# Weight tiles that are a matmul's stationary operand begin 64 bytes further into their buffers

## The chip, the cores and the metric

The kernel runs on one core of a Trainium2 chip. The metric is the device time of one execution in microseconds (us), the median over the runs.

## What is computed

Two transformer blocks over 256 tokens of width 2048, in float32. The first has a stick-breaking attention branch and a latent attention branch with gates, then a feed-forward layer; the second has an attention layer and a retention layer. Nearly all work is multiplying 256 tokens by weight matrices, one after the other:

```python
proj = rms_norm(h, norm_pre_mix) @ w_in                      # 2048 x 8512
q = rms_norm(q_lat, q_norm) @ w_uq;  kv = rms_norm(kv_lat, kv_norm) @ w_ukv
mixed = (g_sb * (sb @ w_o_sb) + g_mla * (mla @ w_o_mla)) @ w_out
gu = rms_norm(h, norm_pre_ffn) @ w_gate_up;  h = h + rms_norm((silu(g) * up) @ w_down)
proj = h @ attn_w_in;  x = layer_norm(ALPHA * x + (o * silu(g)) @ attn_w_out)
proj = x @ ret_w_in;   x = layer_norm(ALPHA * x + (o * silu(g)) @ ret_w_out)
```

## The kernel before

Each weight matrix is read once, in units of 2 x 128 rows by up to 512 columns (512 KB). `run` streams the units: `load` has SyncE (its queue is SPq in the rows) issue the transfer into one of 5 `raw` buffers, up to four units ahead; `split`, three units ahead of use, has ScalarE round the unit to float32r (`whi`) and VectorE compute the rest (`wlo`); four buffers each. Activations are split likewise: `u0` and `u1` (both "u" in rows), `osb`, `omh`/`oml`, `lath`/`latl`, `mh`/`ml`, `oh`/`ol`, `roh`/`rol`. Every product is three float32r matmuls, high by high, high by low and low by high (`mm3`), so TensorE has three matmuls for each pair of 128 x 128 blocks, each behind a load of its own stationary block.

There are two ways to multiply. In `gemm_t` the weights are stationary (128 columns of `whi` or `wlo` are loaded) and 256 columns of activations move through the array; the output is transposed. A full unit is 24 matmuls of 256 columns. In `gemm_n` the activations are stationary and 512 columns of weights move; a unit is 12 matmuls of 512 columns. In rows, the name behind the arrow's first place is the moving operand: `g<-u,whi` is `gemm_t`, `g<-whi,u` is `gemm_n`. `gemm_t` makes the q, k and latent projections of `w_in`, both gates, `w_uq`, `w_o_sb`, `w_o_mla`, the gates of the second attention layer and q and k of retention; `ukv_units` uses each weight tile both ways. The rest, above all the feed-forward layer, is `gemm_n`.

The order of instructions on each engine is the order in which the code issues them; `bg_add` tasks (attention heads, norms) are put between units by `bg_step`.

All large tiles begin at a multiple of 256 bytes in their partition. The `whi` buffers stand at bytes 39,424, 43,520, 47,616 and 51,712, `wlo` from 55,808, `u0` at 72,192, `u1` at 88,576, all of them multiples of 512. `omh`, `oml`, `lath` and `latl` (148,224, 156,416, 191,232 and 201,472) lie 256 bytes off one. The slices that a matmul reads are 512 bytes (stationary), 1,024 or 2,048 bytes (moving) long, and begin at multiples of 256 bytes, too, on both sides.

Two temporaries matter. `diag` makes a diagonal from a vector, for the three row norms of the first block (keys x, q and kv); it has two buffers of 1,024 bytes. `sq0` holds sums of squares at the start, in the place tagged `acc`.

Of the kernel before, what the change touches and what calls it, by code (L numbers as in the profile page):

```python
# [10 lines left out]
F32 = mybir.dt.float32  # L11
F32R = mybir.dt.float32r
# [5 lines left out]
P = 128  # L18
S = 256
# [40 lines left out]
def tile_two_blocks(ctx: ExitStack, tc: tile.TileContext, a, out):  # L60
    nc = tc.nc
# [3 lines left out]
    wp = ctx.enter_context(tc.tile_pool(name="wp", bufs=1))  # L65
    mp = ctx.enter_context(tc.tile_pool(name="main", bufs=1))
# [14 lines left out]
    def gbank():  # L81
        return psg.tile([P, 512], F32, tag="g", name="g")
# [4 lines left out]
    def split2(t, n=2):  # L87
        return t.rearrange("p (a b) -> p a b", a=n)

    def f32(t):  # L90
        return t.bitcast(F32)


    def mm3(o, l, r, start, stop):

        mm(o, l[0], r[0], start, False)
        mm(o, l[0], r[1], False, False)
        mm(o, l[1], r[0], False, stop)

    def mm(o, l, r, start, stop):  # L100
        pe.matmul(out=o, lhsT=l, rhs=r, start=start, stop=stop, skip_group_check=True)  # L101

    def copy(o, i, **k):
        act.activation(out=o, in_=i, func=AF.Copy, **k)  # L104
# [10 lines left out]
    def sub(o, x, y, eng=None):  # L115
        tt(o, x, y, ALU.subtract, eng)
# [26 lines left out]
    class Task:  # L143
        def __init__(self, group, stages, gap, after, at):
            self.group, self.stages, self.gap, self.after, self.at = group, deque(stages), gap, after, at
# [25 lines left out]
    def bg_step():  # L171
        clock[0] += 1
        for _ in range(rate[0]):
            bg_fill()
            t = next((t for t in active if t.at <= clock[0] and not pending(t.after)), None)
            if t is None:
                return
            bg_run(t)
# [34 lines left out]
    units = []  # L213

    class Unit:
        __slots__ = ("srcs", "nk", "nc", "use", "after")

        def __init__(self, srcs, nk, ncol, use, after=False):
            self.srcs, self.nk, self.nc, self.use, self.after = srcs, nk, ncol, use, after

    RAW, SPL, AHEAD = 5, 4, 3
    before_load, before_split = {}, {}
    stream, on_pool = {}, set()

# [5 lines left out]
    def run():  # L230
        raws, parts = {}, {}

        def load(i):
            if i >= len(units):
                return
            before_load.pop(i, lambda: None)()
            u = units[i]
            if u.srcs is None:
                return
            t = wp.tile([P, 2, 512], F32, tag="raw", name="raw", bufs=RAW)  # L240
            for k0, k1, c0, c1, src in u.srcs:
                nc.sync.dma_start(out=t[:, k0:k1, c0:c1], in_=src)
            raws[i] = t

        def split(i):
            if i >= len(units):
                return
            before_split.pop(i, lambda: None)()
            u = units[i]
            if u.srcs is None or i not in raws:  # L250
                return
            t = raws.pop(i)[:, 0:u.nk, 0:u.nc]
            hi = wp.tile([P, 2, 512], F32R, tag="whi", name="whi", bufs=SPL)
            lo = wp.tile([P, 2, 512], F32R, tag="wlo", name="wlo", bufs=SPL)
            copy(hi[:, 0:u.nk, 0:u.nc], t)
            sub(lo[:, 0:u.nk, 0:u.nc], t, f32(hi[:, 0:u.nk, 0:u.nc]), pool if i in on_pool else dve)
            parts[i] = (hi, lo)

        stream["split"] = split
        for i in range(RAW - 1):  # L260
            load(i)
        for i in range(AHEAD):
            split(i)
        for i, u in enumerate(units):
            stream["at"] = i
            if u.srcs is None:
                u.use(None, None)
            load(i + RAW - 1)
            if u.srcs is not None and drip:
                for f in drip.popleft():  # L270
                    f()
            if not u.after:
                split(i + AHEAD)
            if u.srcs is not None:
                u.use(*parts.pop(i))
                if u.after:
                    split(i + AHEAD)
                elif turns and u.use.__name__ != "held":
                    turn_next()
                bg_step()  # L280

    def wsrc(w, k0, nk, c0, ncol):
        return w[k0 * P:(k0 + nk) * P, c0:c0 + ncol].rearrange("(k p) c -> p k c", p=P)

    def gemm_t(w, koff, kblocks, c0, ncol, rhs, evac, srcs=None, blocks=None, before_last=None, lead=None):

        blocks = blocks or [(i * P, min(P, ncol - i * P)) for i in range((ncol + P - 1) // P)]
        st = {}  # L290

        def use_at(k0, nk):
            def use(hi, lo):
                if k0 == 0:
                    st["ps"] = [gbank() for _ in range((len(blocks) + 1) // 2)]
                if k0 + nk == kblocks and before_last:
                    before_last()
                def out_w(b, k):
                    off, m = blocks[b]
                    return (split2(st["ps"][b // 2])[0:m, b % 2, :],  # L300
                            hi[:, k - k0, off:off + m], lo[:, k - k0, off:off + m])

                if k0 == 0 and lead == "w":
                    for x in range(2):
                        for k in range(k0, k0 + nk):
                            for b in range(len(blocks)):
                                o, wh, wl = out_w(b, k)
                                if x:
                                    mm(o, wl, rhs(k)[0], False, False)
                                else:  # L310
                                    mm(o, wh, rhs(k)[0], k == 0 and b % 2 == 0, False)
                                    mm(o, wh, rhs(k)[1], False, False)
                elif lead == "x" and k0 < 4:
                    for k in range(k0, k0 + nk):
                        xh, xl = rhs(k)
                        for b in range(len(blocks)):
                            o, wh, wl = out_w(b, k)
                            mm(o, wh, xh, k == 0 and b % 2 == 0, False)
                            mm(o, wl, xh, False, False)
                        for b in range(len(blocks)):  # L320
                            o, wh, wl = out_w(b, k)
                            mm(o, wh, xl, False, False)
                else:
                    for b in range(len(blocks)):
                        for k in range(k0, k0 + nk):
                            o, wh, wl = out_w(b, k)
                            mm3(o, (wh, wl), rhs(k), k == 0 and b % 2 == 0, k == kblocks - 1)
                if k0 + nk == kblocks:
                    evac(st.pop("ps"))
            return use  # L330

        for k0 in range(0, kblocks, 2):
            nk = min(2, kblocks - k0)
            s = srcs(k0, nk) if srcs else [(0, nk, 0, ncol, wsrc(w, koff + k0, nk, c0, ncol))]
            units.append(Unit(s, nk, ncol, use_at(k0, nk)))

    def gemm_n(w, kblocks, c0, ncol, lhs, evac, koff=0, first=None, last=None):

# [157 lines left out]
    def turn_next():  # L496
        if turns:
            turns.popleft()()
# [17 lines left out]
    def small(name, w=2, bufs=2):  # L516
        return mp.tile([P, w], F32, tag="sm_" + name, name=name, bufs=bufs)

    def diag(r, f):
        dg = mp.tile([P, 2, P], F32, tag="diag", name="diag", bufs=2)  # L520
        stt(dg, ident[:, None, :].to_broadcast([P, 2, P]), f, r[:, :, None].to_broadcast([P, 2, P]),
            ALU.mult, ALU.mult)
        return dg.rearrange("p a b -> p (a b)")
# [10 lines left out]
    def rms_bg(key, get_ps, n, dst):  # L534

        st = {}

        def row():
            v, t = small("v"), small("t")
            st["r"] = small("r", bufs=6)  # L540
            ts(v, get_ps()[:, 0:2], 1.0 / n, ALU.mult, NORM_EPS, ALU.add)
            rsqrt_bg(st["r"], v, t)

        def wide():
            st["d"] = diag(st["r"], 1.0)

        def use():
            o = bbank()
            spread(o, 0, st["d"])
            dst(key, st["r"], o[:, 0:S])  # L550
        return [row, nop, wide, use]
# [20 lines left out]
    p1 = open_phase("p1")  # L572
# [5 lines left out]
    ifr = p1.tile([64, 64], F32, tag="ifr", name="ifr")[:, 0:2]  # L578
    nc.scalar.dma_start(out=cv, in_=a["cv"])
    pool.memset(f32(wz), 0.0)  # L580
    sq0 = p1.tile([P, 2, S], F32, tag="acc", name="sq0")

    copy(small("root"), f32(wz)[:, 0:2])
    warm(22)
# [348 lines left out]
    def ukv_units(p):  # L933
        st = {}
        w = a["w_ukv"]
# [27 lines left out]
                        bg_add("mla%d" % p, mla_head(d, 2 * p + h, h), delay=2)  # L963
            return use
        for k0 in (0, 2):
            units.append(Unit([(0, 2, 0, 512, wsrc(w, k0, 2, p * 512, 512))], 2, 512, use_at(k0)))

    def mla_head(d, head, h):
        st = {}
# [778 lines left out]
```

## Time and profile before

| | |
|---|---|
| median of 3 runs | 2601.6 us (2601.45 to 2601.84) |
| profiled execution, its own time | 2597.73 us |
| its span, first to last instruction | 2595.7 us |
| mean granted clock of TensorE | 0.991 |
| TensorE busy | 2519.6 us (97%) |
| VectorE, ScalarE, GpSimd busy | 1510.1, 1206.2, 232.1 us |
| read from HBM | 458.92 MB, 178 GB/s over the span |

The busy time of TensorE is that of overlapping records: a matmul's record is longer than the distance to the next one's start. How long a matmul keeps the engine is read from the starts.

### The profile page before, as it was taken

To read this page: it belongs to the slowest core of one execution; us is meant where nothing else is said; L and a number is where in the kernel's file an instruction comes from. 1 tells how busy PE (TensorE), PEld (TensorE's weight loads), DVE (VectorE), ACT (ScalarE), POOL (GpSimd) and SP (SyncE) were. 2 spreads that over 40 slices of the span, in tenths; PEclk is the share of its full clock that TensorE was granted. 3 is DMA by queue.
4 is the path that set the end of the run, shared out by engine and by line. 5 is a ranking of instruction groups with operands and counts; after the bars stand their busy time and mean duration, and the time that the engine had idled before them with its cause. 6 is when DMAs were issued, how large, how long until landed. Compare 5 with 4: busy or idle time off the path is not lost.

```text
span 2595.7 us, 36165 instructions
## 1 busy us (share of the span) xinstructions
PE 2519.6 (97%) x14362; PEld 2212.6 (85%) x14362; DVE 1510.1 (58%) x1782; ACT 1206.2 (46%) x1496; POOL 232.1 (9%) x346
## 2 busy tenths in 40 slices
PE   8999999999999999999999899998999999999997
PEld 8999999997778888888888788987889898898785
DVE  7756656556655454445455766766565656565445
ACT  4565554444454444444444445554444444454333
POOL 3012000002000000000000211211110010102000
PEclk9999999999999999999999999999999999999998
DMA  7655555755466666666656454564656556555763
GB/s 228 176 157 157 164 163 174 232 169 180 143 203 187 194 187 193 191 192 193 188 188 194 144 170 146 158 197 156 199 158 184 173 168 185 180 179 156 257 193 115
DMA packets 248889, 465.48 MB, mean 179 GB/s; under 512 B 21328, under 2 KB 31888, under 8 KB 247696
## 3 DMA queue, kind: packets, MB, share of 16 engines
q1 hardware_dynamic: 245312, 448.32, 56.9%
q0 software_dynamic: 2688, 13.63, 1.4%
q8 instruction: 112, 1.84, 0.3%
q10 hardware_dynamic: 720, 1.22, 0.1%
q14 instruction: 57, 0.47, 0.1%
HBM read 458.92 MB, written 4.19 MB: 178 GB/s over the span
## 4 chain that ended last, share of the span: by engine, by line
PE 63%; DVE 3%; POOL 2%; ACT 2%; issue 1%; DMA 1%; POOLq 0%; ACTq 0%; DVEq 0%
PE g L101 60%; PE b L101 2%; DMA raw<-in_ret_w_out_dram 1%; POOL qkraw L107 1%; ACT whi L104 1%; DVE wlo L107 1%; POOL t L107 0%; ACT pp L1357 0%; PE b L1217 0%; POOL z L107 0%; DVE nm L1354 0%; PE b L448 0%; POOL t L417 0%; DVE qkraw L107 0%; PE b L1607 0%
## 5 line engine op out<-in xcount | busy, mean ns | idle before, releaser
L107 DVE TENSOR_TENSOR wlo<-raw,whi 128x1024 fp32r<-128x1024 f32 (+2 forms) x849 | 1053.0, 1250 | 822.8 <-ACT whi L104 817.8
L104 ACT ACTIVATE whi<-raw 128x1024 fp32r<-128x1024 f32 (+2 forms) x852 | 886.9, 1051 | 900.3 <-PE g L101 842.2
L101 PE MATMUL g<-whi,u 128*128 128x512 f32 x3200 | 1009.2, 393 | 0.1
L101 PEld LDWEIGHTS g<-whi,u 128*128 128x128 f32 x3200 | 605.4, 189 | 126.3 <-ACT whi L104 0.6
L101 PE MATMUL g<-wlo,u 128*128 128x512 f32 x1600 | 628.9, 393 | 11.4 <-DVE wlo L107 11.4
L101 PE MATMUL g<-u,whi 128*128 128x256 f32 x3424 | 622.1, 284 | 1.2 <-ACT whi L104 1.2
L101 PEld LDWEIGHTS g<-u,whi 128*128 128x128 f32 x3424 | 532.3, 191 | 2.0 <-ACT whi L104 1.4
L101 PE MATMUL g<-u,wlo 128*128 128x256 f32 x1712 | 483.6, 283 | 8.0 <-DVE wlo L107 8.0
L101 PEld LDWEIGHTS g<-wlo,u 128*128 128x128 f32 x1600 | 303.4, 190 | 76.3 <-DVE wlo L107 15.5
L101 PEld LDWEIGHTS g<-u,wlo 128*128 128x128 f32 x1712 | 326.8, 191 | 9.0 <-DVE wlo L107 9.0
L101 PE MATMUL g<-whi,mh 128*128 128x512 f32 x352 | 137.4, 390 | 0.0
L101 PE MATMUL g<-wlo,mh 128*128 128x512 f32 x352 | 137.0, 389 | 0.0
L101 PE MATMUL g<-whi,ml 128*128 128x512 f32 x352 | 136.0, 389 | 0.0
L101 PE MATMUL g<-wlo,roh 128*128 128x512 f32 x256 | 100.0, 390 | 1.8 <-DVE wlo L107 1.8
L101 PE MATMUL g<-whi,roh 128*128 128x512 f32 x256 | 99.9, 390 | 1.7 <-ACT whi L104 1.7
L101 PE MATMUL g<-whi,rol 128*128 128x512 f32 x256 | 98.7, 389 | 0.0
L107 POOL TENSOR_TENSOR t<-r 128x2 f32<-128x2 f32 (+1 forms) x51 | 21.9, 429 | 654.0 <-DVE r L122 651.3
L101 PEld LDWEIGHTS g<-whi,mh 128*128 128x128 f32 x352 | 66.1, 188 | 13.7
L101 PEld LDWEIGHTS g<-whi,ml 128*128 128x128 f32 x352 | 66.1, 188 | 13.7
L101 PEld LDWEIGHTS g<-wlo,mh 128*128 128x128 f32 x352 | 66.1, 188 | 13.6
L107 POOL TENSOR_TENSOR dacc<-dacc,post_ffn 128x512 f32<-128x512 f32 x6 | 7.6, 1290 | 659.5 <-ACT sqd L438 659.5
L101 PEld LDWEIGHTS g<-wlo,roh 128*128 128x128 f32 x256 | 48.0, 188 | 12.8 <-DVE wlo L107 2.8
(314 smaller groups left out, 2234.5 us busy)
## 6 DMA issues: line engine op xcount, KB each, us to landing
raw<-in_ret_w_in_dram SPq DMA_DIRECT2D x192, 512.0 KB, 4.2
raw<-in_w_gate_up_dram SPq DMA_DIRECT2D x176, 512.0 KB, 3.7
raw<-in_w_in_dram SPq DMA_DIRECT2D x128, 512.0 KB, 4.3
raw<-in_w_down_dram SPq DMA_DIRECT2D x88, 512.0 KB, 4.5
raw<-in_attn_w_in_dram SPq DMA_DIRECT2D x80, 512.0 KB, 3.6
raw<-in_ret_w_out_dram SPq DMA_DIRECT2D x64, 512.0 KB, 4.7
raw<-in_w_out_dram SPq DMA_DIRECT2D x32, 512.0 KB, 4.5
raw<-in_attn_w_out_dram SPq DMA_DIRECT2D x32, 512.0 KB, 4.7
```

The lines of the kernel that those rows point to most:

```text
L101: pe.matmul(out=o, lhsT=l, rhs=r, start=start, stop=stop, skip_group_check=True)
L104: act.activation(out=o, in_=i, func=AF.Copy, **k)
L107: (eng or dve).tensor_tensor(out=o, in0=x, in1=y, op=op)
```

## The change

A weight unit of `gemm_t` or `ukv_units` is split into its `whi` and `wlo` buffers 16 floats, that is 64 bytes, behind the buffer's start. Units of `gemm_n` stay at the start. Each of the eight buffers grows from 4,096 to 4,352 bytes, so that each still begins at a multiple of 256; the 2,048 bytes come from the two `diag` buffers, which now lie in the places of `gate` (key kv) and `sqt` (keys x and q). `sq0` moves into the place of `gate` as well. `u0` and `u1` begin 2,048 bytes later, and all other large tiles stay at multiples of 256. On every engine the same instructions stand in the same order as before; one VectorE multiplication (the first that writes a `gate` tile) waits for one earlier VectorE instruction more.

```diff
     class Unit:
-        __slots__ = ("srcs", "nk", "nc", "use", "after")
+        __slots__ = ("srcs", "nk", "nc", "use", "after", "shift")
...
+    STAT = 16
...
             t = raws.pop(i)[:, 0:u.nk, 0:u.nc]
-            hi = wp.tile([P, 2, 512], F32R, tag="whi", name="whi", bufs=SPL)
-            lo = wp.tile([P, 2, 512], F32R, tag="wlo", name="wlo", bufs=SPL)
+            hi, lo = (wp.tile([P, 1088], F32R, tag=n, name=n, bufs=SPL)[:, u.shift:u.shift + 1024].rearrange(
+                "p (k c) -> p k c", k=2) for n in ("whi", "wlo"))
             copy(hi[:, 0:u.nk, 0:u.nc], t)
...
-            units.append(Unit(s, nk, ncol, use_at(k0, nk)))
+            units.append(Unit(s, nk, ncol, use_at(k0, nk), shift=STAT))
...
-    def diag(r, f):
-        dg = mp.tile([P, 2, P], F32, tag="diag", name="diag", bufs=2)
+    def diag(r, f, tag):
+        dg = p1.tile([P, 2, P], F32, tag=tag, name="diag")
...
-            st["d"] = diag(st["r"], 1.0)
+            st["d"] = diag(st["r"], 1.0, "gate" if key == "kv" else "sqt")
...
-    sq0 = p1.tile([P, 2, S], F32, tag="acc", name="sq0")
+    sq0 = p1.tile([P, 2, S], F32, tag="gate", name="sq0")
...
-            units.append(Unit([(0, 2, 0, 512, wsrc(w, k0, 2, p * 512, 512))], 2, 512, use_at(k0)))
+            units.append(Unit([(0, 2, 0, 512, wsrc(w, k0, 2, p * 512, 512))], 2, 512, use_at(k0), shift=STAT))
```

## Rows read from the trace of the kernel before

**Rows 1.** The page: busy us, share of the span and instructions of each engine.

```profile
PE 2519.6 (97%) x14362; PEld 2212.6 (85%) x14362; DVE 1510.1 (58%) x1782; ACT 1206.2 (46%) x1496; POOL 232.1 (9%) x346
```

**Rows 2.** The chain that ended last: shares of the span by engine.

```profile
PE 63%; DVE 3%; POOL 2%; ACT 2%; issue 1%; DMA 1%; POOLq 0%; ACTq 0%; DVEq 0%
```

**Rows 3.** Groups by form, TensorE: out<-moving,stationary, stationary size, moving size, count | busy us, mean ns.

```profile
L101 PE MATMUL g<-whi,u 128*128 128x512 f32 x3200 | 1009.2, 393 | 0.1
L101 PE MATMUL g<-u,whi 128*128 128x256 f32 x3392 | 616.9, 284 | 1.2 <-ACT whi L104 1.2
L101 PE MATMUL g<-u,wlo 128*128 128x256 f32 x1696 | 479.1, 283 | 8.0 <-DVE wlo L107 8.0
...
L101 PE MATMUL g<-lath,whi 128*128 128x256 f32 x104 | 29.6, 285 | 0.0
...
L101 PE MATMUL g<-u,whi 128*64 128x256 f32 x32 | 5.9, 277 | 0.0
```

**Rows 4.** Timeline, TensorE in a `gemm_t` stretch: start us, us, operation, count.

```profile
517.17 0.28 PE L101 MATMUL g<-omh,wlo 128*128 128x256 f32 x1
517.29 0.40 PE L101 MATMUL g<-u,whi 128*128 128x256 f32 x2
...
518.37 0.40 PE L101 MATMUL g<-u,whi 128*128 128x256 f32 x2
```

**Rows 5.** Timeline, TensorE in a `gemm_n` stretch.

```profile
899.87 0.62 PE L101 MATMUL g<-whi,u 128*128 128x512 f32 x2
...
901.23 0.62 PE L101 MATMUL g<-whi,u 128*128 128x512 f32 x2
```

**Rows 6.** Five stretches: busy us (count) by engine, granted clock, DMA share, GB/s.

```profile
core 0: us, PE busy (x) PEld busy (x) DVE busy (x) ACT busy (x) POOL busy (x), PEclk, DMA share, GB/s
8.00:63.00 55.00, 47.04 (x383) 45.98 (x382) 42.79 (x43) 24.42 (x32) 23.71 (x26) 1.00 0.73 229
517.40:540.20 22.80, 22.80 (x192) 22.80 (x191) 12.11 (x13) 8.44 (x8) 0.00 (x0) 1.00 0.63 187
1844.00:1889.60 45.60, 45.60 (x382) 45.60 (x381) 25.48 (x26) 21.68 (x25) 0.00 (x0) 1.00 0.67 202
980.00:1090.00 110.00, 110.00 (x487) 91.06 (x487) 49.79 (x41) 45.75 (x47) 0.00 (x0) 1.00 0.62 195
688.50:691.50 3.00, 3.00 (x9) 2.35 (x8) 3.00 (x4) 1.99 (x3) 1.88 (x1) 0.50 0.00 0
```

**Rows 7.** Timeline, TensorE in the stretch at half clock.

```profile
688.43 0.63 PE L101 MATMUL g<-wlo,u 128*128 128x512 f32 x1
...
691.42 1.18 PE L101 MATMUL g<-whi,u 128*128 128x512 f32 x4
```

**Rows 8.** Timeline, TensorE where 64 stationary columns are loaded.

```profile
218.45 0.40 PE L101 MATMUL g<-u,whi 128*64 128x256 f32 x2
...
218.80 0.39 PE L101 MATMUL g<-u,whi 128*64 128x256 f32 x2
...
219.14 0.40 PE L101 MATMUL g<-u,whi 128*128 128x256 f32 x2
```

**Rows 9.** Timeline, TensorE in a `gemm_t` unit behind a wait.

```profile
31.24 0.40 PE L101 MATMUL g<-u,whi 128*128 128x256 f32 x2
31.49 0.28 PE L101 MATMUL g<-u,wlo 128*128 128x256 f32 x1
31.60 0.40 PE L101 MATMUL g<-u,whi 128*128 128x256 f32 x2
31.84 0.28 PE L101 MATMUL g<-u,wlo 128*128 128x256 f32 x1
```

**Rows 10.** Timeline, TensorE in a `gemm_n` unit behind a wait.

```profile
710.10 0.62 PE L101 MATMUL g<-whi,u 128*128 128x512 f32 x2
710.57 0.40 PE L101 MATMUL g<-wlo,u 128*128 128x512 f32 x1
```

**Rows 11.** What reads and writes `diag`: duration ns min/median/max, first and last start.

```profile
L125 DVE SCALAR_TENSOR_TENSOR diag<-kc,r x3: 416/417/425, 51.4 to 259.9; 128x256 f32<-128x256 f32 x3
```

More of the change, by code (lines that the diff above doesn't have):

```diff
@@ L215, in tile_two_blocks, with __init__ @@
     class Unit:
-        __slots__ = ("srcs", "nk", "nc", "use", "after")
-        def __init__(self, srcs, nk, ncol, use, after=False):
-            self.srcs, self.nk, self.nc, self.use, self.after = srcs, nk, ncol, use, after
+        __slots__ = ("srcs", "nk", "nc", "use", "after", "shift")
+        def __init__(self, srcs, nk, ncol, use, after=False, shift=0):
+            self.srcs, self.nk, self.nc, self.use, self.after, self.shift = srcs, nk, ncol, use, after, shift
     RAW, SPL, AHEAD = 5, 4, 3
+    STAT = 16
     before_load, before_split = {}, {}
```

## The prediction

> **What bounds the kernel now.** I read the page first, then whole stretches, then the starts of single matmuls. TensorE is busy 97% of the span [rows 1], and the chain that ended last runs over it for 63%, with no other engine above 3% [rows 2]. In a late `gemm_t` stretch TensorE is busy in all of its 45.60 us, with VectorE at 25.48 and ScalarE at 21.68; the `gemm_n` stretch from 980 looks the same [rows 6]. So in steady stretches nothing but the pace of TensorE's own instructions sets the time, and a change that adds and removes no instruction can act only through that pace.
>
> The busy time hides the pace, because records overlap: a 256-column matmul is recorded with 283 to 285 ns, a 512-column one with 393 [rows 3]. The starts give it. In `gemm_t` ten matmuls start between 517.17 and 518.37: 1.20 us, 120.0 ns each [rows 4]. In `gemm_n` six start between 899.87 and 901.23: 226.7 ns each [rows 5].
>
> [...]
>
> [...]
>
> **Does it depend on how the two reads lie to each other?** In time, yes. Behind a wait, tiles at the same kind of addresses give other distances: 0.25 us for two matmuls from 31.24 to 31.49 (125 each, as far as a row's 10 ns tell), then 0.11 for one, then 0.24 for two [rows 9]; with 512 columns, 0.47 us for two (235 each) [rows 10]. Some matmuls later it is 120.0 and 226.7 again. A fixed cost would not do that. In address, the trace is silent: every stationary and moving slice begins at a multiple of 256 bytes. Pairs that lie 256 bytes apart modulo 512 (`lath` as moving operand) go at the same pace as `u`, 285 against 284 ns of record [rows 3], so if an address counts, it is within 256 bytes, and there the change moves one of the two reads by a quarter.
>
> **The change part by part.** It removes and adds no instruction.
>
> The moved reads: 3,392 + 1,696 matmuls of `u` with full blocks, 48 with 64-column blocks, 384 of `osb`, 384 of `omh` and `oml`, 312 of `lath` and `latl` [rows 3]: 6,216. `gemm_n` keeps its 226.7 ns; its stationary operand and its moving weights stay where they were.
>
> [...]
>
> What swallows gain: from 8 to 63 us TensorE is busy only 47.04 of 55.00 us [rows 6], waiting for weights, `xs` and their splits, and its 383 matmuls there would only wait longer. 6,216 - 383 = 5,833 are left, at 6.7 ns each 39 us. Elsewhere supply suffices: a `gemm_t` unit would take 24 x 113.3 ns = 2.72 us, and a `gemm_n` unit takes 12 x 226.7 ns = 2.72 us for the same 512 KB, which runs without idle at 195 GB/s [rows 6]. ScalarE and VectorE have half of the stretch free.
>
> The splits write the same elements in one run of 1,024, 64 bytes further. I cost them at nothing; the cover is the free half of ScalarE and VectorE, and if one became longer by a tenth, VectorE's 25.48 us would be 28 of 45.60. The larger buffers only move `u0` and `u1` by 2,048 bytes, still at a multiple of 256.
>
> The diagonals: three instructions of 0.42 us [rows 11], which now wait for former users of other places (sums of squares, long done). The first `gate` tile waits for the last reader of a diagonal, which stands ahead of it anyway. I take nothing; the bound is 3 x 0.42 = 1.3 us, if all three slid onto the path. Nothing gets faster by it.
>
> The sum: -39 us and +0 to +1.3, so about -38 us. Against the profiled execution's 2597.7 us this is 2559.7. The median of the runs stands 3.9 us above that execution, so 2563.6, rounded to **2564 us**.
>
> **Rivals.**
> [...]
> *Nothing happens: the change doesn't do what it says.* [...] The varying distances of [rows 9, 10] then come from time alone, which 64 bytes don't alter. Time 2601.6. [...]
> *Slower.* The 64 bytes could bring the reads into a worse position than the present one, such as that of the 125 ns behind a wait [rows 9, 10]. The place is each of the same matmuls; at 122 to 125 ns it costs 2 to 5 ns x 6,216 = 12 to 31 us: 2614 to 2633. A stationary slice that crosses a multiple of 512 bytes, which none did before, would be one way. It decides from 0.8 ns per matmul on, which is 5.2 us.
>
> **How the numbers follow.** 0.2%, or 5.2 us, is about what a measurement of this kernel can tell from no change. About half of the surplus gone (110 to 117 ns, 2543 to 2584 us): 0.40. All or nearly all gone: 0.12. Nothing: 0.30. Slower: 0.18. The likeliest gives 2564, with its own range of 2543 to 2584. Faster by over 0.2% is 0.40 + 0.12 = 0.52, within 0.2% 0.30, slower 0.18. The range of eight in ten takes in "nothing" with its 5 us at the top and most of "all gone" at the bottom: 2526 to 2606; it leaves out the slower case.
>
> **What would show it.** Right: ten starts of a `gemm_t` stretch span 1.13 us in place of 1.20, `gemm_n` keeps 1.36 for six; the stretch with 45.60 us shrinks to about 43 with its GB/s up by 6%; TensorE waits longer in the first 63 us, and nowhere else. Wrong: starts at 120.0 ns as before (nothing), a `gemm_n` distance that moves (then the 2,048 bytes of `u`, or the buffers' distance of 4,352, matter, not the 64), or a saving given back in waits for `wlo`, `whi` or transfers. The prediction is wrong above all if the address within 256 bytes has no say, or if it has and the sign is the other one.

## The result: 2573.7 us, and the profile after

| | before | after |
|---|---|---|
| median, us | 2601.5 (2600.5 to 2601.8, 4 runs) | 2573.7 (2572.7 to 2577.4, 4 runs) |
| profiled execution, its own time and span, us | 2597.73, 2595.7 | 2574.57, 2572.9 |

The ratio is 0.9896, with a 95% interval of 0.9879 to 0.9913: 27.8 us faster. A second profiled execution of the same kernel, on another chip, took 2569.58 us (span 2567.9); there the ratio was 0.9912 (0.9899 to 0.9926).

The page of after has the same instructions and the same picture as [rows 1, 2], TensorE at 97% with 24.7 us less to do:

```profile
PE 2494.9 (97%) x14362; PEld 2187.6 (85%) x14362; DVE 1509.1 (59%) x1782; ACT 1206.4 (47%) x1496; POOL 232.3 (9%) x346
...
PE 66%; DVE 2%; POOL 2%; ACT 1%; DMA 1%; issue 1%; POOLq 0%; ACTq 0%; DVEq 0%
```

Four windows of after, with the columns of [rows 6]: the start, two `gemm_t` stretches, a `gemm_n` stretch.

```profile
8.00:63.00 55.00, 48.15 (x388) 46.81 (x387) 43.67 (x44) 24.75 (x32) 23.36 (x26) 0.97 0.73 234
500.00:545.60 45.60, 45.60 (x405) 45.60 (x404) 26.34 (x27) 19.59 (x21) 0.00 (x0) 1.00 0.63 192
1830.00:1865.00 35.00, 35.00 (x299) 35.00 (x298) 20.59 (x21) 16.05 (x18) 0.00 (x0) 1.00 0.63 191
980.00:1090.00 110.00, 110.00 (x487) 91.09 (x486) 49.64 (x41) 46.74 (x48) 0.00 (x0) 1.00 0.62 193
```

45.60 us now hold 405 matmuls of 256 columns and not 382; the 35 us from 1830 hold 299, which is 390 in 45.60. `gemm_n` has its 487 as before. TensorE is busy throughout, so nothing waits. The starts say the same more exactly; the timeline of TensorE in after, at three places:

```profile
515.79 0.39 PE L101 MATMUL g<-u,whi 128*128 128x256 f32 x2
...
518.17 0.39 PE L101 MATMUL g<-u,whi 128*128 128x256 f32 x2
...
1839.81 0.40 PE L101 MATMUL g<-u,whi 128*128 128x256 f32 x2
...
1842.28 0.40 PE L101 MATMUL g<-u,whi 128*128 128x256 f32 x2
...
892.78 0.62 PE L101 MATMUL g<-whi,u 128*128 128x512 f32 x2
...
895.50 0.39 PE L101 MATMUL g<-whi,u 128*128 128x512 f32 x1
```

The rows between are left out; counted with them, 21 distances lie between the first two: 2.38 us, 113.3 ns each. 21 lie between the next two: 2.47 us, 117.6 ns each. Twelve of 512 columns take 2.72 us, 226.7 ns each, as in [rows 5]. So `gemm_n` is untouched, and **`gemm_t` has two paces**, with the same tiles at the same kind of addresses. Taken over all steady distances of the trace, `gemm_t` went from 119.9 ns to 115.5 (about 6,000 distances in each); about 3,200 of these stand in stretches that settle at 113.3, most of them within five matmuls, and about 2,700 in stretches at 117.8. A stretch keeps one pace for hundreds of matmuls: 1,030 in a row at 113.3 from 440.4 us, 383 at 117.8 from 1825.7. Which pace it keeps is not fixed by the program: one stretch of 118 distances, the same instructions on the same tiles, has 113.3 in this execution and 117.8 in the second one. The timeline of TensorE there, first in this execution, then in the second:

```profile
232.37 0.39 PE L101 MATMUL g<-u,whi 128*128 128x256 f32 x2
...
245.29 0.39 PE L101 MATMUL g<-u,whi 128*128 128x256 f32 x2
```

```profile
232.23 0.40 PE L101 MATMUL g<-u,whi 128*128 128x256 f32 x2
...
245.66 0.40 PE L101 MATMUL g<-u,whi 128*128 128x256 f32 x2
```

114 distances each, in 12.92 and in 13.43 us.

### The profile page after: what moved, and what is told of

It reads as the page before. It is cut to its first block, busy times and chain, and to the rows that moved or that the text cites. A ratio compares the mean times of both kernels' runs of the same rounds, so it can differ in the third digit from the quotient of the medians.

```text
span 2572.9 us, 36166 instructions
## 1 busy us (share of the span) xinstructions
PE 2494.9 (97%) x14362; PEld 2187.6 (85%) x14362; DVE 1509.1 (59%) x1782; ACT 1206.4 (47%) x1496; POOL 232.3 (9%) x346
## 4 chain that ended last, share of the span: by engine, by line
PE 66%; DVE 2%; POOL 2%; ACT 1%; DMA 1%; issue 1%; POOLq 0%; ACTq 0%; DVEq 0%
PE g L101 62%; PE b L101 2%; POOL qkraw L107 1%; DMA raw<-in_ret_w_out_dram 1%; PE b L1218 0%; POOL z L107 0%; PE b L449 0%; ACT pp L1358 0%; DVE wlo L107 0%; PE b L1333 0%; PE b L1369 0%; PE b L1608 0%; POOL t L107 0%; DVE z L107 0%; DMA gn<-in_again_dram 0%
## 5 line engine op out<-in xcount | busy, mean ns | idle before, releaser
L101 PE MATMUL g<-u,whi 128*128 128x256 f32 x3424 | 603.7, 281 | 0.9 <-ACT whi L104 0.9
L101 PEld LDWEIGHTS g<-u,whi 128*128 128x128 f32 x3424 | 522.2, 189 | 1.8 <-ACT whi L104 1.1
L101 PE MATMUL g<-u,wlo 128*128 128x256 f32 x1712 | 477.4, 280 | 6.9 <-DVE wlo L107 6.7
L101 PEld LDWEIGHTS g<-u,wlo 128*128 128x128 f32 x1712 | 321.2, 188 | 7.9 <-DVE wlo L107 7.9
```

## The experiments

The theory after the result: the distance between two matmuls depends on where the stationary read stands to the moving read, modulo 256 bytes, and in some places also on how the stretch was entered. The rivals: the larger buffers, the moved `u0` and `u1` or the diagonals are what helped; the weights' address counts by itself; a stretch's pace comes from what it reads, or from load or real waits, not from its entry.

### 1. Everything but the 64 bytes

```diff
-    STAT = 16
+    STAT = 0
```

> The change with a shift of 0: larger buffers, shared temporaries and u moved by 2,048 bytes stay, the 64 bytes are taken away. If the 64 bytes are the cause, the time is that of before, 2601.5 us within 3, and gemm_t goes at 120.0 ns per matmul. If the other parts of the change bring the gain, it is 2574, with gemm_t at 113 to 118.

2597.5 us against 2599.0 on that chip, ratio 1.000 (0.999 to 1.0009); `gemm_t` at 119.9 ns. The shared places, the larger buffers and the moved `u` do nothing that can be measured: the 64 bytes are the cause.

### 2. Bare matmuls, one offset after another

The whole computation is left out, and the output is a copy of the input; the program only repeats matmuls with one stationary tile (`sa` to `sr`, read from 0, 4, 8, 16, 32, 48, 64, ... 240 bytes behind a multiple of 256).

```python
for t, o in zip(st, OFFS):                      # straight behind 512 columns
    seg("c", zero, mc[:, 0:512], 14)
    seg("a", t[:, o:o + P], ma[:, 0:256], 40)
for t, o in zip(st, OFFS):                      # behind a wait
    copy(mb, xs[:, 0, 0:640])
    seg("b", t[:, o:o + P], mb[:, 0:256], 40)
for t, o in zip(st, OFFS):
    seg("d", t[:, o:o + P], md[:, 0:512], 40)
```

> Leaves out the whole computation: x is copied to the output, and TensorE runs stretches of 40 equal matmuls whose stationary slice begins 0, 4, 8, 16, 32, ... 240 bytes past a multiple of 256, with 256 and with 512 moving columns, and some whose moving slice is shifted by 0, 64, 128 and 192 bytes. If the address of one read against the other counts (theory), the distance of two starts is 120.0 ns at 0 bytes and falls to 113 to 118 at 64, other values in between, and a shift of both by 64 bytes gives 120 again. If only the address of the stationary slice counts, a shift of both by 64 gives 113 to 118 like that of the stationary one alone. If time alone counts and the gain of the change is from elsewhere (rival), all offsets give the same distance. For 512 columns the theory leaves open whether 226.7 falls at some offset; the rival says it never does.

Timeline of TensorE; a row is a whole segment, so its distance is the next row's start minus its own, divided by the count. `sa` is 0 bytes, `sc` 8, `sg` 64, `sk` 128.

```profile
28.83 4.96 PE L48 MATMUL ga<-ma,sa 128*128 128x256 f32 x40
33.62 3.37 PE L48 MATMUL gc<-mc,sa 128*128 128x512 f32 x14
...
44.76 4.79 PE L48 MATMUL ga<-ma,sc 128*128 128x256 f32 x40
49.39 3.38 PE L48 MATMUL gc<-mc,sa 128*128 128x512 f32 x14
...
76.46 4.88 PE L48 MATMUL ga<-ma,sg 128*128 128x256 f32 x40
81.18 3.37 PE L48 MATMUL gc<-mc,sa 128*128 128x512 f32 x14
...
108.24 4.96 PE L48 MATMUL ga<-ma,sk 128*128 128x256 f32 x40
113.04 3.35 PE L48 MATMUL gc<-mc,sa 128*128 128x512 f32 x14
...
168.50 4.95 PE L48 MATMUL gb<-mb,sa 128*128 128x256 f32 x40
...
203.65 4.81 PE L48 MATMUL gb<-mb,sg 128*128 128x256 f32 x40 [0.89 <-ACT mb L33]
...
272.98 9.27 PE L48 MATMUL gd<-md,sa 128*128 128x512 f32 x40
282.09 9.45 PE L48 MATMUL gd<-md,sb 128*128 128x512 f32 x40
...
328.59 9.49 PE L48 MATMUL gd<-md,sg 128*128 128x512 f32 x40
337.92 9.44 PE L48 MATMUL gd<-md,sh 128*128 128x512 f32 x40
```

Behind 512 columns, 40 matmuls of 256 take 4.79 us at 0 bytes, 4.63 at 8, 4.72 at 64 and 4.80 at 128: 119.8, 115.8, 118.0 and 120.0 ns. Behind a wait the segment at 64 bytes is shorter, 4.81 us with its last record, against 4.95 at 0. The distances of the settled part of each segment (the last 27 of its 39), from starts to the nanosecond:

| offset, bytes | 0 | 8 | 16 to 48 | 64 | 80 to 112 | 128 to 160 | 192 |
|---|---|---|---|---|---|---|---|
| 256 columns, behind 512 | 120.0 | 115.6 | 118.3 to 118.4 | 117.8 | 117.4 to 120.0 | 119.9 to 120.0 | 117.8 |
| 256 columns, behind a wait | 120.0 | 115.6 | 117.8 to 118.4 | **113.3** | 117.3 to 120.2 | 120.0 to 120.1 | **113.3** |
| 512 columns | **226.7** | 230.8 | 233.3 | 233.3 | 232.0 to 234.3 | 233.3 to 233.5 | 228.9 |

Of the offsets that the table leaves out (4, 176, 208, 224 and 240 bytes), none came below 116.6 ns for 256 columns or below 228.4 for 512.

Three things follow. Both paces of `gemm_t` in the kernel are here, at one offset; besides the entry, only the moving tile differs (`ma`, `mb`), and both begin at a multiple of 256 bytes. For 512 columns 0 bytes are the best of these places, and 64 cost 6.7 ns ((337.92 - 328.59) / 40 = 233.3). And in further segments, where the moving operand was shifted, 64 bytes on the moving side with 0 on the other went like 192 on the stationary side (117.8 and 228.9), 64 on both like 0 on both (120.0 and 226.7): the distance between the two counts, modulo 256, and not where either lies. Of the eight pairs two don't fit exactly, both with the moving operand 128 bytes ahead: they gave 232.4 ns for 512 columns where 128 on the stationary side gave 233.5, and one of them 118.5 for 256 columns in place of 120.0. Whether that is the entry again was not tested.

### 3. The 64 bytes elsewhere

First all weights, those of `gemm_n` too, where they are the moving operand; then `u0` and `u1` in place of the weights.

```diff
-        def __init__(self, srcs, nk, ncol, use, after=False, shift=0):
+        def __init__(self, srcs, nk, ncol, use, after=False, shift=16):
```

> The change with every weight unit shifted by 64 bytes, so that in gemm_n the moving weights lie 64 bytes past the stationary activations. gemm_t is as in the change. If a distance of 64 bytes helps whichever of the two reads is ahead, gemm_n's 226.7 ns fall to 220 (6.7 ns on 7,054 matmuls, 47 us, 2527 us). If it helps only where the stationary slice is the shifted one, gemm_n stays at 226.7 and the time at 2574. If the sign matters and this one is bad, gemm_n rises and the time lies above 2574, by 7 us for each ns.

```diff
-    STAT = 16
+    STAT = 0
...
-        U[0] = mp.tile([P, KD, S], F32R, tag="u0", name="u0")
-        U[1] = mp.tile([P, KD, S], F32R, tag="u1", name="u1")
+        U[:] = [mp.tile([P, KD * S + 64], F32R, tag=n, name=n)[:, 16:16 + KD * S].rearrange(
+            "p (k t) -> p k t", k=KD) for n in ("u0", "u1")]
```

> The weights unshifted, u0 and u1 64 bytes further in. gemm_t with u then has its moving slice 64 bytes past the stationary one, and gemm_n with u has its stationary slice 64 bytes past the moving one, 4,800 matmuls. If the distance of the two reads counts with its sign, gemm_n with u falls below 226.7 as gemm_t did in the change (up to 6.7 ns, 32 us, 2570 us) and gemm_t with u is open. If only the stationary slice's own address counts, gemm_t stays at 120.0 and gemm_n with u falls. If only 256 moving columns are sensitive, gemm_n stays at 226.7 and the time at 2601.

All weights: 2588.4 us, ratio 0.9958 (0.9945 to 0.997). `u` alone: 2615.2, ratio 1.0069 (1.0054 to 1.0084). The timelines of TensorE in a `gemm_n` stretch, first of the kernel with all weights shifted, then of that with `u` shifted:

```profile
892.95 0.62 PE L101 MATMUL g<-whi,u 128*128 128x512 f32 x2
...
896.38 0.62 PE L101 MATMUL g<-whi,u 128*128 128x512 f32 x2
```

```profile
899.76 0.63 PE L101 MATMUL g<-whi,u 128*128 128x512 f32 x2
...
903.96 0.39 PE L101 MATMUL g<-whi,u 128*128 128x512 f32 x1
```

15 distances in 3.43 us, 228.7 ns; and 18 in 4.20 us, 233.3 ns. These are the sweep's 228.9 (192 bytes) and 233.3 (64 bytes). In the second kernel 4,800 matmuls of `gemm_n` with `u` pay 6.7 ns, 32 us, while 5,136 of `gemm_t` gain only 2.4 (119.9 to 117.5), 12 us: 20 us to lose, and 16 were measured. The `gemm_t` matmuls of `osb`, `omh`/`oml` and `lath`/`latl`, where neither operand is shifted in this kernel, keep 120 ns. None of the three outcomes written down for `u` had a slower `gemm_n`; the one that came for all weights, a distance that rises, had been written down with its price. It shows in the kernel that no tile's own address decides, but the two together, and why only the stationary weights are shifted.

### 4. Other offsets, and the entry by itself

Again bare matmuls without the computation: ten ways from 512 columns at 0 bytes into 60 matmuls of 256 columns at 64, then finer offsets, 64 stationary columns and float32 operands.

```python
for kick, m in zip(kicks, ks):                  # kick: nothing, or one or two short matmuls
    seg("c", zero, mc[:, 0:512], 14)
    kick()
    seg("a", far, m[:, 0:256], 60)
```

> Bare matmuls; the whole computation is left out and the output is a copy of the input, so only distances between starts inside the segments count. Part one: ten times, 14 matmuls of 512 columns with all operands at a multiple of 256 bytes, then nothing or one or two short odd matmuls, then 60 of 256 columns with the stationary operand 64 bytes on (moving operands ka to kj). Theory A (the 64-byte position has two steady patterns, 113.3 and 117.8 ns, and which one a stretch takes is settled by how the first matmul of it lies in time to the last of the 512-column ones): with nothing between, 117.8 ns, as behind 512 columns in the first sweep; with some of the odd matmuls between, 113.3 ns for all 60, with others 117.8, and no third value. Rival B (the pattern is settled by the load on TensorE over a longer time, or by a real wait): all ten at 117.8 ns, since none of them has a wait. Part two, finer offsets behind 512 columns: by A, offsets near 64 bytes give 117.8 or 113.3 ns, and 8 to 12 bytes stay at about 115.6; a value below 113 anywhere would be a better place than the change's. [...] Part four, float32 operands, whose columns take longer: the distance is the same at offsets 0 and 64 if the moving operand is read too slowly there to collide.

Timeline of TensorE, read as in experiment 2:

```profile
27.58 7.23 PE L55 MATMUL ga<-ka,z 128*128 128x256 f32 x60
34.65 3.36 PE L55 MATMUL gc<-mc,z 128*128 128x512 f32 x14
...
79.23 0.40 PE L55 MATMUL gb<-mc,z 128*128 128x512 f32 x1
79.47 6.97 PE L55 MATMUL ga<-kf,z 128*128 128x256 f32 x60
86.27 3.36 PE L55 MATMUL gc<-mc,z 128*128 128x512 f32 x14
...
226.26 4.71 PE L55 MATMUL gd<-ma,sm 128*128 128x256 f32 x40
230.81 3.37 PE L55 MATMUL gc<-mc,z 128*128 128x512 f32 x14
234.02 4.96 PE L55 MATMUL gd<-ma,sn 128*128 128x256 f32 x40
238.82 3.36 PE L55 MATMUL gc<-mc,z 128*128 128x512 f32 x14
...
257.70 4.71 PE L55 MATMUL ge<-mh,z 128*64 128x256 f32 x40
262.25 3.36 PE L55 MATMUL gc<-mc,z 128*128 128x512 f32 x14
265.44 4.93 PE L55 MATMUL ge<-mh,z 128*64 128x256 f32 x40
270.21 3.38 PE L55 MATMUL gc<-mc,z 128*128 128x512 f32 x14
```

With nothing between, 60 matmuls take 7.07 us, 117.8 ns each; with a single 512-column matmul at 64 bytes between, 6.80 us, 113.3 ns each. Of the ten entries four settled at 113.3 (that one; two of 64 columns; one float32 matmul; two of 256 columns at 224 bytes), six at 117.8, and none at a third value. No wait was needed: the entry theory held, and the rival of load or waits fell. The rival of what a stretch reads falls by the stretch shown with the result, which takes either pace with the same reads. Of the finer offsets 76 bytes (`sm`: 4.55 us for 40) and 88 came to 113.3 behind 512 columns after four matmuls; 84 (`sn`: 4.80 us for 40) stayed at 120.0, 24 was the worst with 122.0, and none came below 113.3.

Two forecasts failed. Offsets near 64 bytes were to give 117.8 or 113.3 ns, but 60 gave 119.4, 68 and 72 gave 118.3 to 118.4, and 52 gave 120.0. And with 64 stationary columns, where 64 bytes were to be the cheaper place, 0 bytes gave 113.3 once settled and 64 bytes 119.0 (4.55 and 4.77 us for 40). With float32 operands (the trace has two records for each of these matmuls) the records start 215.8 ns apart at 0 and at 64 bytes alike (8.79 us for 40 records at both, the last one's length included), so a matmul of 256 columns takes 431.6 ns there; between these two places there is no difference, as forecast.

### 5. 128, 8, 76 and 84 bytes in the kernel

Each is the change with one number altered (`STAT` is 32, 2, 19 or 21); the change itself ran once more beside the last two.

> The change with 128 bytes in place of 64. Theory A (the place of the stationary read against the moving read, modulo 256 bytes, sets the pace, as the first sweep showed: 120.0 ns at 128 as at 0): the time of before, ratio to it 0.998 to 1.002, gemm_t at 120 ns. Rival (any place that parts the two reads, or a place off the buffers' starts, is as good): ratio 0.988 to 0.991 as with 64 bytes, 113 to 118 ns.

> The change with 8 bytes in place of 64. Theory A: 115.6 ns for each gemm_t matmul, whatever ran before it (the first sweep gave 115.56 behind 512 columns and behind a wait alike). That is 4.3 ns off 120 on 5,833 matmuls, so some 25 us: 2574 to 2578 against 2599, ratio 0.990 to 0.992, the same as with 64 bytes, but with one pace in all stretches instead of two. Rival (64 bytes act because they are a quarter of 256, and small offsets don't carry from bare matmuls to the kernel): 118 to 120 ns, ratio 0.995 to 1.0.

> The change with 76 bytes in place of 64; nothing else differs. In the sweep of bare matmuls this offset came to 113.33 ns after four matmuls even behind 512 columns, where 64 bytes stayed at 117.78. Theory A (two steady patterns at 64 bytes, of which the slow one can be left when the place is less regular): gemm_t at 113.3 to 114 ns in all stretches, the long ones behind gemm_n too; 2,570 matmuls gain 4.4 ns more than with 64 bytes, 11 us: 2560 to 2566, ratio to before 0.984 to 0.988. Rival (the sweep's value at this offset was a chance of its entry): 117 to 118 ns, the time of 64 bytes or worse, ratio 0.989 or more.

> As with 76 bytes: in the sweep 84 bytes went to 113.33 ns as well, after four matmuls behind 512 columns. Theory A: 113.3 to 114 ns in all stretches, 2560 to 2566 us, ratio to before 0.984 to 0.988. Rival (chance of the entry): ratio 0.989 or more. If one of 76 and 84 bytes holds and the other not, only that one is a place without the slow pattern.

> The change itself (64 bytes) beside the two other places on the same chip, for a comparison with them. All theories: 2570 to 2576 us, ratio to before 0.988 to 0.991, about 2,570 gemm_t matmuls at 117.8 ns and the others at 113.3.

| bytes | us | ratio to before | steady `gemm_t`, ns |
|---|---|---|---|
| 128 | 2595.8 | 0.9989 (0.9979 to 0.9998) | 119.3 |
| 8 | 2577.3 | 0.9922 (0.9906 to 0.9937) | 115.8 |
| 76 | 2571.6 | 0.9902 (0.9888 to 0.9915) | 114.8 |
| 84 | 2599.5 | 1.0007 (0.9998 to 1.0015) | 120.0 |
| 64 | 2573.7 | 0.9912 (0.9899 to 0.9926) | 115.5 |

The timelines of TensorE near 520 us for 8 bytes, then for 84:

```profile
519.99 0.39 PE L101 MATMUL g<-u,whi 128*128 128x256 f32 x2
...
522.42 0.39 PE L101 MATMUL g<-u,whi 128*128 128x256 f32 x2
```

```profile
519.79 0.40 PE L101 MATMUL g<-u,whi 128*128 128x256 f32 x2
...
522.31 0.41 PE L101 MATMUL g<-u,whi 128*128 128x256 f32 x2
```

21 distances each: 115.7 and 120.0 ns. 128 bytes put the two reads apart as well, by half of 256, and give next to nothing: parting them is not what helps. The little that they give comes from a second pace here too: three late stretches of 334 matmuls run at 118.7 ns, the other long ones at 120.0. 8 bytes gain nearly what 64 do, with one pace in all stretches, as the sweep said. 84 bytes were put up by a misreading of the sweep: their expectation gives them the value that stands at 88. The sweep has 120.0 for 84, and 120.0 is what the kernel does with them, so this run, meant as a gain, shows a forecast of the sweep come true in the other direction. 76 bytes gave what was expected behind every 512-column entry, and yet came out 6 us above the range expected of it, for this reason (timeline of TensorE with 76 bytes):

```profile
1944.79 0.39 PE L101 MATMUL g<-u,whi 128*128 128x256 f32 x2
...
1948.87 0.39 PE L101 MATMUL g<-u,whi 128*128 128x256 f32 x2
...
1949.21 1.04 PE L1608 MATMUL b<-kc,ron 128*128 128x128 f32 x8
...
1950.81 0.40 PE L101 MATMUL g<-u,whi 128*128 128x256 f32 x2
...
1954.77 0.40 PE L101 MATMUL g<-u,whi 128*128 128x256 f32 x2
```

Up to 1948.87 the stretch runs at 113.3 ns. Then eight transposes of a `bg_add` task come between two units, and behind them the same stretch runs at 120.0 (33 distances in 3.96 us), for 334 matmuls; likewise from 2093 and 2236 us.

### 6. The transposes moved out of the stretch

```diff
-                bg_add("tr%d" % h, [nop, nop, tr], gap=1)
+                bg_add("tr%d" % h, [nop] * (17 if h % 2 else 2) + [tr], gap=1)
```

This puts them 15 units later, into the `gemm_n` stretch behind; once with 76 bytes, once with 64 as the control.

> 76 bytes, and the eight transposes that stood behind the second unit of three retention gemm_t stretches come 15 units later, in the gemm_n stretch behind it; nothing is left out. Theory A (the pattern is settled at the entry of a stretch; at 76 bytes an entry behind 512 columns leads to 113.3 ns, the entry behind those transposes to 120.0): the 3 x 334 matmuls that ran at 120.0 ns from 1950, 2093 and 2236 us on now keep 113.3, 6.7 us less than with 76 bytes alone: 2564 to 2567 us, ratio to before 0.987 to 0.9885. Rival (those stretches are slow for what they read, not for how they are entered): 120.0 ns there as before, ratio 0.990.

> The control: 64 bytes with the same transposes moved. Theory A: at 64 bytes an entry behind 512 columns leads to 117.8 ns, and the stretches from 1954, 2097 and 2239 us had 117.8 ns already, so nothing moves: 2572 to 2576 us, ratio 0.990 to 0.991. Rival (the transposes themselves cost time where they stood, and moving them is what gains): 2566 to 2570, at the same 117.8 ns.

With 76 bytes: **2565.8 us, ratio 0.9874 (0.9857 to 0.989)**. With 64: 2576.9, ratio 0.9909 (0.9895 to 0.9924). The timeline of TensorE in the same stretch, with 76 bytes:

```profile
1942.68 0.39 PE L101 MATMUL g<-u,whi 128*128 128x256 f32 x2
...
1950.84 0.39 PE L101 MATMUL g<-u,whi 128*128 128x256 f32 x2
```

72 distances in 8.16 us: 113.3 ns, through the place where the transposes stood. All eleven stretches of over 100 matmuls run at it, and the mean of all steady distances is 113.7. In the control those three stretches keep 117.8, and the time stays within the scatter of the other runs with 64 bytes: moving the transposes gains nothing by itself. So the entry sets the pace, and the version with 76 bytes, 11 us under the control on the same chip, is the best that was found. Its time is close to the 2564 forecast for the change.

## Why the prediction was right, and where it was off

It forecast 2564 us, faster, "about half of the surplus gone"; 2573.7 is inside its range and inside the likeliest case's own (2543 to 2584). The surplus is an estimate from the rows: 512 columns take 226.7 ns and 256 take 120.0 [rows 4, 5], so 256 columns more take 106.7, and 13.3 are left over in both. At the granted clock of 0.50, 512 columns take 427 ns [rows 6, 7], four times 106.7. No run shows a matmul of 256 columns at 106.7 ns.

**That the pace of TensorE alone bounds it**: right in the main. Matmul by matmul, the steady distances of `gemm_t` add up to 26.2 us less than before, in either profiled execution of the change. In the profiled execution of before and the first one of after, the first 512-column matmul behind the first block's `gemm_t` work starts at 587.48 and 567.01 us: 20.5 us saved by there. The last `gemm_t` stretch ends at 2300.20 and 2278.73: 21.5. In between, some 3 us were lost in the passage from the feed-forward to the attention layer, where the granted clock was 0.95 from 1420 to 1495 us and 0.93 from 1495 to 1520, and before had 0.98 from 1440 to 1515 and 1.00 from 1515 to 1540; the second execution (21.7 and 25.6 us saved at the two places, mean granted clock 0.991 as in before) lost under half a us, so that is scatter. A little was given back in waits for GpSimd's work: TensorE waited 10.2 us for `qkraw` (9.8 in the second execution) where before it waited 8.5, and in the first execution 1.4 us for a diagonal in place of 0.5.

**That an address within 256 bytes has a say**: right, and shown by experiments 1 and 5. The rival "nothing happens" fell. With the same instructions in the same order, 64 bytes on one operand changed 120.0 to 113.3 or 117.8 ns (256 columns) and 226.7 to 233.3 (512 columns). By what means the two reads act on each other, no run shows. The prediction took from the records' durations that 256 bytes make no difference (285 and 284 ns), though it had said that durations hide the pace; the starts agree (120.0 ns for `lath` before).

**The picture of two reads that are parted by a quarter**: not borne out. It does not say why 64 bytes slow 512 columns down (226.7 to 233.3 ns), why they slow matmuls with 64 stationary columns (113.3 to 119.0), why 128 bytes do next to nothing (120.0 to 119.3), or why one place has two paces. That the surplus at 0 bytes is alike for 256 and 512 columns, 13.3 ns by the estimate above, does not show one cause: the two behave oppositely when moved. What the runs show in its place is that the starts fall into a repeating pattern, which the distance of the two operands and the entry settle; what that pattern is made of stays open.

**The price, 113.3 ns**, from which the 6.7 ns of the sum come: the author's choice, the shortest distance of 256-column matmuls in the trace of before, with 64 stationary columns (three from 218.80 to 219.14 [rows 8]). It was right for half of the matmuls, to a tenth of a nanosecond; the term was mis-sized because it was taken as one price for all. No run of the change shows 6.7 ns on all 5,833 matmuls: the runs showed 113.3 ns for about half and 117.8 for the others. No run gives a reason for 113.3 either, so that the value is met exactly is luck. The mean is 115.5, so the gain is 4.4 ns and not 6.7 on 5,833 matmuls: 26 us and not 39. Experiment 6 ran nearly all of them at 113.3 and saved 35 us against the 2600.8 of its own chip, where the sum had 38.

**"Its 383 matmuls there would only wait longer"** (the first 63 us): wrong, by little. 388 matmuls start in that window where there were 383, and the `gemm_t` stretch at 85.65 us begins 1.6 us sooner. TensorE is idle there for 6.85 us where it was 7.96; it was elsewhere that it came to wait longer. With 5,833 x 4.4 ns = 25.7 this makes 27.3, against 27.8 measured here and 23.9 on the second chip (2597.6 to 2573.7); that it meets the first so closely is chance.

**Supply, splits, diagonals at nothing**: right as far as the runs tell: experiment 1 has all of them without the 64 bytes, at ratio 1.000 and with 0.5 us of waiting for a diagonal as before, and the long `gemm_t` stretches of after have TensorE busy throughout.

**The other rivals**: that all or nearly all of the surplus goes (106.7 ns, by the estimate above) fell; no offset that was tried came below 113.3 with 256 columns. "Slower" is real at other places, not at this one: 122.0 ns at 24 bytes in bare matmuls, and 233.3 for `gemm_n` (experiment 3). The way to it that the prediction named, a stationary slice across a multiple of 512 bytes, is none: with the change every full stationary slice of `whi` or `wlo` in `gemm_t` begins 64 bytes past a multiple of 256, is 512 bytes long and so crosses one, and `gemm_t` got faster. Of the signs named ahead, the ten starts in 1.13 us came in half of the stretches, and the stretch that [rows 6] show from 1844, whole, went from 46.07 us to 45.23 at 117.8 ns, and to 43.5 only with 76 bytes. GB/s rose with the pace. The windows of after shown above are not the stretches of [rows 6]; over one whole stretch, the longest, before and after show 202 and 213 GB/s, 5% more at 113.3 ns:

```profile
454.10:577.60 123.50, 123.50 (x1032) 123.50 (x1031) 62.09 (x61) 51.29 (x60) 0.00 (x0) 1.00 0.64 202
440.50:557.00 116.50, 116.50 (x1030) 116.50 (x1029) 61.72 (x61) 51.02 (x59) 0.00 (x0) 1.00 0.66 213
```

## What to carry to other kernels

Read TensorE's pace from the starts, not from the records (120.0 ns against 284 here); it can depend on where the stationary and the moving slice stand to each other within 256 bytes (113.3 to 122.0 ns for 256 columns here), and a shift of one operand is a cheap thing to try. Try it by operand and by width: the 64 bytes that help 256 moving columns (120.0 to 113.3 or 117.8) hurt 512 (226.7 to 233.3). And look at a long stretch's pace behind each kind of entry, since a background task or a switch of width can fix it for hundreds of matmuls: eight transposes fixed 120.0 ns for 334 (76 bytes, experiment 5), a switch from 512 columns 117.8 for 383 (64 bytes, from 1825.7 us).

## What was not expected of the hardware

- One sequence of instructions has two steady paces, 113.3 and 117.8 ns at 64 bytes, 113.3 and 120.0 at 76, and stays in the one that it enters: 1,030 matmuls in a row. One odd matmul ahead switched it from 117.8 to 113.3 (experiment 4), and the same stretch of one program took either pace in two executions.
- The paces are exact: at a granted clock of 1.00 the distances of after go 114, 113, 113 ns again and again from 445 us on, those of before are 120 ns but for 6 of 291 (119 or 121) from 1850 to 1885, and those of 512 columns in before go 227, 226, 227 from 900. 117.8 is the average of a pattern of nine that repeats: 118, 117, 119, 117, 118, 118, 117, 118, 118 ns in after from 1840 us.
- 8 bytes, far less than a quarter of 256, gain nearly as much as 64 in the kernel (ratio 0.9922 and 0.9912), and behind every entry that was measured (115.6 ns in bare matmuls behind 512 columns and behind a wait, 115.8 in the kernel).
- Whether other places, or a mixture of places by stretch, come below 113.3 ns with 128 stationary columns was not tried beyond the offsets named.
